# Background weights by Pool's queue into three places, with four smaller edits, in a two-layer hybrid trunk

## The chip, the cores and the metric

The kernel runs as one program on one core of a Trainium2 chip. The metric is the device time of one execution in microseconds; before the change it was measured three times. TensorE (PE) does the matrix products, VectorE (DVE) and ScalarE (ACT) the elementwise work, GpSimd (POOL) a few small operations, and SyncE (SP) issues the transfers. Each engine runs its own instructions in order.

## The reference

Two layers of one mixer over 256 latent tokens and 256 context tokens of width 2048, batch 1, all in float32. The second layer needs the context only for keys and values. Cut to what matters here (the rotary positions of q and k are left out):

```python
for l in range(2):
    shift, scale, gate = split(silu(c) @ w_mod[l] + b_mod[l])        # and the same of c_ctx for the context
    h = rmsnorm(x, norm_g[l]) * (1 + scale) + shift
    q, k, v, g_att, u_pool, g_pool, a, b, g_conv = split(h @ w_in[l])  # 2048 -> 6656
    # 8 heads, each with two softmaxes over context and latent keys
    p = softmax(q @ k.T * 64 ** -0.5)
    o = (p[0] - lam * p[1]) @ v
    y_att = rmsnorm(o, subln_g) * (1 - lam_init) * silu(g_att)
    y_pool = multiscale_pool(u_pool) * silu(g_pool)
    y_conv = conformer_conv(a, b) * silu(g_conv)
    x = x + gate * (concat(y_att, y_pool, y_conv) @ w_out[l])
return rmsnorm(x, final_g)
```

## The kernel before

Activations lie with the channels on the 128 partitions and the tokens (512, or 256 in layer 1) along the free side: the residual is 16 tiles `s0` to `s15`. To keep float32 accuracy each operand is split into a high part in the float32r form and a low part that is the rest (ScalarE casts, VectorE subtracts), and each product is three matmuls: high by high, low by high, high by low. The names end in `h` and `l`: `hh`, `hl` are the normalised input, `in_q_h`, `in_q_l` weights of a chunk of q, from the loaded `in_q_r`. The input projection is done chunk by chunk (`b0 a0 q0 k0 v0 u0 b1 ...`, 256 columns each, 16 tiles of the inner dimension), each into two banks of PSUM (`ps_q`, `ps_v`, ...).

**The first stage.** The x tiles are loaded, squared on ScalarE and added up on VectorE (`add_squares`); TensorE sums over the channels (`rms_sum`, line 178), GpSimd takes the power -1/2 (line 145), TensorE spreads the root over the partitions (line 160), and ScalarE copies it (`rstd`). Meanwhile the modulation of layer 0 (shift and scale) is made on TensorE from 512 KB pieces `wm` (line 336, `modacc`); each finished pair is turned by a small matmul (`modt`) and finished on VectorE (`modsum`, `mod`). Each tile of `h`, `hh`, `hl` then feeds the first three chunks at once (`ps_first`, three held pairs of banks), as their weights `first_*` come. The order within this stage is written out by hand: inside `in_order()` each engine keeps the order of the code.

**The background.** The gates of layer 0 and the whole modulation of layer 1 are made on VectorE, by `mod_on_dve`: 8 units of 1024 columns in 16 pieces each, 128 loads `mraw` of 128x1024 and 224 multiply-accumulates `macc` (line 370 the first of a unit, line 372 the others; two for each piece where latent and context rows are both wanted, one otherwise). Its places rotate under the tag `mraw`, `MRAW` of them; the first stage's `wm` pieces use the same tag for two of every eight. A load for piece n+1 is issued when the macc of piece n is written, into the place that macc n-1 has left:

```python
        for n in range(MRAW - 1):
            load(n)
        yield 0.0
        for n, (l, u, both, k) in enumerate(pieces):
            load(n + MRAW - 1)
            raw = raws.popleft()
```

**Attention** (`attention`, one pair of heads) is a generator too. After the scores, `softmax` takes the negative maximum (`mx`, line 634), two exponentials with sums (line 640), the reciprocal `r` of both sums (line 644), multiplies the second by minus lambda (line 645), scales the first part on ScalarE (line 648) and adds the second on VectorE (line 649); TensorE then transposes the result `ex` into `atx` (line 684). At the end of a pair the squares of the head outputs are summed (`ssq`) and rooted by three Newton steps on VectorE (`arw`, lines 152 to 154) into a kept tile `arv`. Later, when the gate chunk `ga` is projected, `gate_att` splits that root, spreads it with eight matmuls (`ar`), multiplies the head by it (line 761) and by the silu of the gate (line 762).

A scheduler interleaves the generators with the projection chunks: each `yield` gives the microseconds of VectorE work that a step is taken to be, and every projection step of `FULL` hands that much out. So the numbers at the `yield`s set where on VectorE the maccs and the attention's steps stand.

## Time and profile before

| what | value |
|---|---|
| three runs | 1498.68, 1493.88, 1495.42 us, median 1495.42 |
| profiled execution | 1502.84 us, its span 1501.0 us |
| mean granted TensorE clock | 0.992 |
| TensorE busy | 1452.5 us, 97% |
| VectorE busy | 1112.8 us, 74% |
| ScalarE busy | 650.2 us, 43% |
| GpSimd busy | 9.0 us, 1% |
| transfers | 258.9 MB, nearly all by SyncE's queue |

The time of a run is that of the whole execution; the span of the profile is from the first instruction to the last, and all times below count from its start. The profiled execution is a run of its own, 7.4 us above the median of the other three. "Busy" of TensorE counts the time that a matmul is in its pipeline, at whatever clock.

### The profile page before, as it was taken

Reading aid. Unit: us, or ns where it says so; the run is one execution under the profiler, and the core shown is the slowest. Engines: PE = TensorE matmul, PEld = TensorE weight load, DVE = VectorE, ACT = ScalarE, POOL = GpSimd, SP = SyncE. Lnnn points to the kernel's source line nnn. Section 1 sums busy time; section 2 is a strip of 40 time slices with the busy share of each in tenths; the row PEclk is TensorE's granted clock in tenths of the full one; section 3 lists DMA queues with packets and bytes.
Section 4 is the critical chain, followed back from the end, with each engine's and each line's share of the span. In section 5 each row is a group of like instructions: output and inputs, shape, how many; then the busy total and the mean of one; then the engine's idle time right before and its main releaser. Section 6 shows DMA issues by size and latency. Waiting matters only on the chain.

```text
span 1501.0 us, 23277 instructions
## 1 busy us (share of the span) xinstructions
PE 1452.5 (97%) x9196; PEld 1241.8 (83%) x9196; DVE 1112.8 (74%) x1641; ACT 650.2 (43%) x1245; POOL 9.0 (1%) x46
## 2 busy tenths in 40 slices
PE   4999999999999999999999999999999999999997
PEld 3567977897797977888888889988989897999997
DVE  4446999997549865879898964998995567475655
ACT  4224363227546363332433242635545545464543
POOL 0000000000000000000000000000000000000000
PEclk9999999999999999999999999999999999999998
DMA  8995226432234613655667761436733264245553
GB/s 332 397 391 221 81 88 202 148 110 74 74 112 146 202 60 113 221 195 203 209 213 250 243 222 55 142 114 216 265 113 124 79 227 161 99 134 178 187 183 113
DMA packets 75855, 258.90 MB, mean 172 GB/s; under 512 B 8800, under 2 KB 11104, under 8 KB 75744
## 3 DMA queue, kind: packets, MB, share of 16 engines
q1 hardware_dynamic: 75456, 257.14, 49.2%
q8 instruction: 72, 1.18, 0.3%
q14 instruction: 39, 0.32, 0.1%
q10 hardware_dynamic: 288, 0.26, 0.1%
HBM read 255.27 MB, written 2.10 MB: 171 GB/s over the span
## 4 chain that ended last, share of the span: by engine, by line
PE 83%; DVE 7%; DMA 4%; issue 3%; ACT 2%; SPq 0%; POOL 0%; POOLq 0%; DVEq 0%; ACTq 0%
PE ps_o L236 16%; PE ps_k L236 12%; PE ps_ga L236 9%; PE ps_v L227 7%; PE ps_q L236 6%; PE ps_gc L236 5%; PE ps_gp L236 4%; PE ps_first L236 4%; PE ps_b L236 3%; PE ps_u L236 3%; PE ps_a L236 3%; DMA mraw<-in_w_mod 3%; PE modacc L336 2%; DVE s L479 2%; DVE macc L372 1%
## 5 line engine op out<-in xcount | busy, mean ns | idle before, releaser
L372 DVE SCALAR_TENSOR_TENSOR macc<-mraw,c_sb,macc 128x1024 f32<-128x1024 f32 x210 | 262.6, 1280 | 32.2 <-DMA mraw<-in_w_mod 31.5
L236 PE MATMUL ps_o<-yh,out_h 128*128 128x512 f32 (+1 forms) x448 | 151.7, 339 | 0.0
L236 PE MATMUL ps_o<-yl,out_h 128*128 128x512 f32 (+1 forms) x448 | 151.6, 338 | 0.0
L236 PE MATMUL ps_o<-yh,out_l 128*128 128x512 f32 (+1 forms) x448 | 151.6, 338 | 0.0
L227 PE MATMUL ps_v<-in_v_h,hh 128*128 128x256 f32 x512 | 145.2, 284 | 0.0
L227 PE MATMUL ps_v<-in_v_h,hl 128*128 128x256 f32 x512 | 144.8, 283 | 0.0
L227 PE MATMUL ps_v<-in_v_l,hh 128*128 128x256 f32 x512 | 144.3, 282 | 0.0
L479 DVE SCALAR_TENSOR_TENSOR s<-cu,vec,s 128x512 f32<-128x512 f32 (+1 forms) x240 | 136.5, 615 | 0.5
L205 ACT CAST out_h<-out_r 128x1024 fp32r<-128x1024 f32 x56 | 58.8, 1050 | 111.5 <-PE ps_o L236 97.2
L236 PE MATMUL ps_k<-hh,in_k_h 128*128 128x512 f32 x256 | 102.9, 402 | 1.9 <-ACT ex L640 1.0
L236 PE MATMUL ps_k<-hl,in_k_h 128*128 128x512 f32 x256 | 102.1, 399 | 0.0
L236 PE MATMUL ps_k<-hh,in_k_l 128*128 128x512 f32 x256 | 101.8, 398 | 0.0
L227 PEld LDWEIGHTS ps_v<-in_v_l,hh 128*128 128x128 f32 x512 | 96.7, 189 | 0.3
L227 PEld LDWEIGHTS ps_v<-in_v_h,hh 128*128 128x128 f32 x512 | 96.7, 189 | 0.3
L227 PEld LDWEIGHTS ps_v<-in_v_h,hl 128*128 128x128 f32 x512 | 96.4, 188 | 0.0
L236 PEld LDWEIGHTS ps_o<-yl,out_h 128*128 128x128 f32 x448 | 84.3, 188 | 9.9
L236 PEld LDWEIGHTS ps_o<-yh,out_h 128*128 128x128 f32 x448 | 84.3, 188 | 9.9
L236 PEld LDWEIGHTS ps_o<-yh,out_l 128*128 128x128 f32 x448 | 84.3, 188 | 9.8
L206 DVE TENSOR_TENSOR out_l<-out_r,out_h 128x1024 fp32r<-128x1024 f32 x56 | 68.1, 1223 | 32.1 <-ACT out_h L205 30.7
L236 PE MATMUL ps_ga<-hh,in_ga_h 128*128 128x512 f32 (+1 forms) x256 | 87.2, 340 | 1.0 <-ACT ex L640 1.0
L236 PE MATMUL ps_ga<-hl,in_ga_h 128*128 128x512 f32 (+1 forms) x256 | 87.0, 340 | 0.0
L236 PE MATMUL ps_ga<-hh,in_ga_l 128*128 128x512 f32 (+1 forms) x256 | 87.0, 340 | 0.0
(407 smaller groups left out, 3708.2 us busy)
## 6 DMA issues: line engine op xcount, KB each, us to landing
mraw<-in_w_mod SPq DMA_DIRECT2D x128, 512.0 KB, 4.3
wm<-in_w_mod SPq DMA_DIRECT2D x64, 512.0 KB, 8.5
out_r<-in_w_out SPq DMA_DIRECT2D x56, 512.0 KB, 4.0
in_k_r<-in_w_in SPq DMA_DIRECT2D x32, 512.0 KB, 4.4
in_v_r<-in_w_in SPq DMA_DIRECT2D x32, 512.0 KB, 3.4
in_ga_r<-in_w_in SPq DMA_DIRECT2D x32, 512.0 KB, 3.8
in_q_r<-in_w_in SPq DMA_DIRECT2D x28, 512.0 KB, 3.5
in_u_r<-in_w_in SPq DMA_DIRECT2D x16, 512.0 KB, 3.4
```

The lines of the kernel that those rows point to most:

```text
L205: nc.scalar.copy(out=hi, in_=raw)
L206: nc.vector.tensor_sub(out=lo, in0=raw, in1=hi.bitcast(F32))
L227: nc.tensor.matmul(o, lhsT=a[:, ts], rhs=b[:, j, :], start=f and n == 0 and tt % 2 == 0, stop=e and n == 2, skip_group_check=True,)
L236: nc.tensor.matmul(ps[:, nt, t0:t1], lhsT=a[:, j, ns], rhs=b[:, t0:t1], start=f and n == 0, stop=e and n == 2,)
L336: nc.tensor.matmul(acc[c : c + 32, :n], lhsT=sc32[:, k, :], rhs=raw[:, j, :], start=k < 4, stop=k >= KT - 4, skip_group_check=True,)
L372: nc.vector.scalar_tensor_tensor(out=acc[:, r, :], in0=raw, scalar=sc[:, k, r : r + 1], in1=acc[:, r, :], op0=ALU.mult, op1=ALU.add)
L479: nc.vector.scalar_tensor_tensor(out=acc, in0=u[:, :nq, j : j + TL], scalar=w[:, j : j + 1], in1=acc, op0=ALU.mult, op1=ALU.add)
```

## The change

1. **Loads of the background** go from SyncE's queue to GpSimd's, and `MRAW` is 3 instead of 2: two loads are written ahead, and a load waits for the macc two pieces before its own but one (load n+2 for macc n-1). The third `mraw` place is there for the first stage's `wm` too.
2. **Heads' normalisation**: the split of the root, its eight matmuls and the product with the head move from `gate_att` to the end of `attention`, which gets a step of 1.2; `gate_att` keeps the silu and one product.
3. **Softmax**: the second reciprocal is multiplied by minus lambda on ScalarE, ahead of the scaling there, no longer on VectorE.
4. **First stage**: `ident` and `vec0` are loaded behind the tenth x tile; squares are added in pairs of tiles (six adds of 128x1024, three of 128x512, before fifteen of 128x512); sums and spread use a held bank of `ps_first`; TensorE does the sums, three modulation pieces, the spread, the fourth piece.
5. **Its end**: `take` (the GLU, pooling or rotary steps that follow a chunk) of the first three chunks is called right behind the last product of each.

```diff
-MRAW = 2
+MRAW = 3
...
-                nc.sync.dma_start(out=raw, in_=w_mod[6 * l + u - 4, k])
+                nc.gpsimd.dma_start(out=raw, in_=w_mod[6 * l + u - 4, k])
...
-        nc.vector.tensor_scalar(out=r[:, 1, :], in0=r[:, 1, :], scalar1=L.neglam, scalar2=None, op0=ALU.mult)
+        nc.scalar.activation(r[:, 1, :], r[:, 1, :], AF.Copy, scale=L.neglam)
...
-        v = one.tile([P, TL], F32, tag=f"arv{p}", name=f"arv{l}_{p}")[:, :nh]
+        work = tmp(f"arw{l}_{p}")
+        v, a, y = work[:, :nh], work[:, TL : TL + nh], tmp(f"ary{l}_{p}")[:, :nh]
         nc.vector.tensor_scalar(out=v, in0=b, scalar1=1.0 / P, scalar2=EPS, op0=ALU.mult, op1=ALU.add)
...
-    def gate_att(L, p, ps):
...
-        split_act(hi, lo, L.arstd[p])
+        split_act(hi, lo, v)
+        yield 4.0
         for h in range(2):
...
+            o = L.y[2 * p + h]
+            nc.vector.scalar_tensor_tensor(out=o, in0=o, scalar=L.subg, in1=r, op0=ALU.mult, op1=ALU.mult)
+        L.arstd[p] = True
+        yield 1.2
...
-            nc.vector.scalar_tensor_tensor(out=y, in0=y, scalar=L.subg, in1=r, op0=ALU.mult, op1=ALU.mult)
             nc.vector.tensor_tensor(out=y, in0=y, in1=g[:, :n], op=ALU.mult)
...
+    def last_product(k, i):
+        product(k, i)
+        if k == KT - 1:
+            take(L, ORDER[i], held[i])
...
             nc.sync.dma_start(out=s[k], in_=xT[k])
+            if k == 9:
+                small_loads()
...
-        add_squares(s, sq_acc, "xsq")
+        both = mp.tile([P, 2, 1024], F32, tag="macc", name="xsq", bufs=1)[:, 0, :]
+        for k in range(0, KT - 2, 2):
+            q = both if k == 0 else at.tile([P, 1024], F32, tag=("vh", "vl", "ah", "al")[k // 2 % 4], name=f"xsq{k}")
+            for i in range(2):
+                nc.scalar.activation(q[:, i * T : (i + 1) * T], s[k + i], AF.Square)
+            if k:
+                nc.vector.tensor_tensor(out=both, in0=both, in1=q, op=ALU.add)
...
+        y = rstd_of([sq_acc], 4, 1.0 / D, "rms0", held[2][:, 0, :])
         steps = mod_on_pe(0)
-        next(steps)
-        next(steps)
-        y = rstd_of([sq_acc], 4, 1.0 / D, "rms0")
+        for _ in range(3):
+            next(steps)
         finishes.popleft()()
-        next(steps)
-        next(steps)
-        r0 = spread(y, "rms0")
+        r0 = spread(y, "rms0", held[2][:, 1, :])
```

**Where instructions stand now.** VectorE in layer 1 ahead of the first softmax of head 4 (`mxx_4_0`, `rx_4_0`), before; `macc_5` is the unit with its pieces `mraw_5_0` to `mraw_5_15`, the rest are splits of weights:

```order
L372 SCALAR_TENSOR_TENSOR macc_5_11107<-mraw_5_7_11232,c_sb,macc_5_11107 128x1024
L206 TENSOR_TENSOR in_q_3_l<-in_q_3_r,in_q_3_h 128x1024
L372 SCALAR_TENSOR_TENSOR macc_5_11107<-mraw_5_8_11235,c_sb,macc_5_11107 128x1024
L634 TENSOR_REDUCE mxx_4_0_11343<-sx_4_0_11336 128x2
L372 SCALAR_TENSOR_TENSOR macc_5_11107<-mraw_5_9_11292,c_sb,macc_5_11107 128x1024
L206 TENSOR_TENSOR in_q_2_l<-in_q_2_r,in_q_2_h 128x1024
L634 TENSOR_REDUCE mxx_4_1_11391<-sx_4_1_11384 128x2
L372 SCALAR_TENSOR_TENSOR macc_5_11107<-mraw_5_10_11295,c_sb,macc_5_11107 128x1024
L644 RECIPROCAL rx_4_0_11349<-ssx_4_0_11346 128x2
L206 TENSOR_TENSOR in_k_0_l<-in_k_0_r,in_k_0_h 128x1024
L645 TENSOR_SCALAR rx_4_0_11349<-rx_4_0_11349,neglam_8163 128x1
```

The same place after the change. Piece 13 stands ahead of the reciprocal `rx_4_0` where piece 10 did, and line 645's product is gone from VectorE. Ahead of the layer's first reciprocal it is piece 9 where it was piece 7:

```order
L374 SCALAR_TENSOR_TENSOR macc_5_11110<-mraw_5_10_11295,c_sb,macc_5_11110 128x1024
L215 TENSOR_TENSOR vl_2_11305<-ps_v_1_11042,vh_2_11304 128x1024
L208 TENSOR_TENSOR in_q_3_l<-in_q_3_r,in_q_3_h 128x1024
L374 SCALAR_TENSOR_TENSOR macc_5_11110<-mraw_5_11_11298,c_sb,macc_5_11110 128x1024
L636 TENSOR_REDUCE mxx_4_0_11346<-sx_4_0_11339 128x2
L208 TENSOR_TENSOR in_q_2_l<-in_q_2_r,in_q_2_h 128x1024
L374 SCALAR_TENSOR_TENSOR macc_5_11110<-mraw_5_12_11301,c_sb,macc_5_11110 128x1024
L374 SCALAR_TENSOR_TENSOR macc_5_11110<-mraw_5_13_11642,c_sb,macc_5_11110 128x1024
L646 RECIPROCAL rx_4_0_11352<-ssx_4_0_11349 128x2
L636 TENSOR_REDUCE mxx_4_1_11394<-sx_4_1_11387 128x2
L651 SCALAR_TENSOR_TENSOR ex_4_0_11348<-ex_4_0_11348,rx_4_0_11352 128x512
```

VectorE at the end of the first stage, before: the last tile's `h_15`, its second modulation, and `hl_15`, with the lambda's steps and the first macc behind it.

```order
L411 SCALAR_TENSOR_TENSOR h_15_1278<-s_106,mod_118,rstd_305 128x256 x2
L206 TENSOR_TENSOR in_k_3_l<-in_k_3_r,in_k_3_h 128x1024
L326 TENSOR_REDUCE modsum_15_1308<-modt_15_1306 128x2
L290 TENSOR_TENSOR mod_118<-modsum_15_1308,vec_84 128x2
L422 SCALAR_TENSOR_TENSOR hl_15_152<-h_15_1278,mod_118,hh_15_151 128x256 x2
L828 TENSOR_TENSOR lam_1339<-lam_1339 128x128
L830 TENSOR_REDUCE lams_1342<-lam_1339 128x2
L370 TENSOR_SCALAR macc_4_2285<-mraw_4_0_2281,c_sb 128x1024
```

The same after: two line-372 products and one macc (line 374) stand between `h_15` and `hl_15`, three maccs more behind it, and lambda's steps have moved back.

```order
L413 SCALAR_TENSOR_TENSOR h_15_1264<-s_106,mod_115,rstd_279 128x256 x2
L372 TENSOR_SCALAR macc_4_2318<-mraw_4_0_2312,c_sb 128x1024
L208 TENSOR_TENSOR in_k_3_l<-in_k_3_r,in_k_3_h 128x1024
L328 TENSOR_REDUCE modsum_15_1294<-modt_15_1292 128x2
L372 TENSOR_SCALAR macc_4_2318<-mraw_4_0_2312,c_sb 128x1024
L292 TENSOR_TENSOR mod_115<-modsum_15_1294,vec_84 128x2
L374 SCALAR_TENSOR_TENSOR macc_4_2318<-mraw_4_1_2314,c_sb,macc_4_2318 128x1024
L424 SCALAR_TENSOR_TENSOR hl_15_149<-h_15_1264,mod_115,hh_15_148 128x256 x2
L374 SCALAR_TENSOR_TENSOR macc_4_2318<-mraw_4_1_2314,c_sb,macc_4_2318 128x1024
L374 SCALAR_TENSOR_TENSOR macc_4_2318<-mraw_4_2_2316,c_sb,macc_4_2318 128x1024 x2
```

TensorE at the start, before (`wm_0_0` and `wm_0_1` are pieces of the first modulation, `ps_first` with `first_0` the first product):

```order
L336 MATMUL modacc_0_240<-wm_0_0_172,sc_115 32x128 x8
L336 MATMUL modacc_0_240<-wm_0_1_174,sc_115 32x128 x8
L178 MATMUL rms_sum<-ones,sq_acc 128x1 x4
L323 MATMUL modt_0_271<-ident,modrow_0_261 128x128
L336 MATMUL modacc_0_277<-wm_0_0_176,sc_115 32x128 x8
L336 MATMUL modacc_0_277<-wm_0_1_178,sc_115 32x128 x8
L160 MATMUL rms_rstd<-ident,rms_v 128x128 x4
L323 MATMUL modt_0_310<-ident,modrow_0_298 128x128
L236 MATMUL ps_first_153<-hh_0_121,first_0_0qh 128x512
```

After: the sums (line 180) come first and the spread (line 162) stands behind three pieces and the turn.

```order
L180 MATMUL ps_first_152<-ones,sq_acc 128x1 x4
L338 MATMUL modacc_0_235<-wm_0_0_171,sc_112 32x128 x8
L338 MATMUL modacc_0_235<-wm_0_1_173,sc_112 32x128 x8
L338 MATMUL modacc_0_258<-wm_0_0_175,sc_112 32x128 x8
L325 MATMUL modt_0_269<-ident,modrow_0_256 128x128
L162 MATMUL ps_first_152<-ident,rms_v 128x128 x4
L338 MATMUL modacc_0_258<-wm_0_1_177,sc_112 32x128 x8
L325 MATMUL modt_0_296<-ident,modrow_0_291 128x128
L238 MATMUL ps_first_150<-hh_0_118,first_0_0qh 128x512
```

## Rows read from the trace of the kernel before

**Rows 1.** The page, part 1: busy time, share of the span and instructions of each engine.

```profile
PE 1452.5 (97%) x9196; PEld 1241.8 (83%) x9196; DVE 1112.8 (74%) x1641; ACT 650.2 (43%) x1245; POOL 9.0 (1%) x46
```

**Rows 2.** The page, part 4: the chain that ended last, shares of the span.

```profile
PE 83%; DVE 7%; DMA 4%; issue 3%; ACT 2%; SPq 0%; POOL 0%; POOLq 0%; DVEq 0%; ACTq 0%
```

**Rows 3.** Windows: busy time of each engine, then granted clock, DMA share, GB/s.

```profile
50.00:75.00 25.00, 22.86 (x186) 14.51 (x179) 11.55 (x27) 7.68 (x15) 0.00 (x0) 1.00 1.02 406
150.00:200.00 50.00, 49.47 (x317) 43.62 (x315) 49.86 (x68) 19.04 (x27) 0.00 (x0) 1.00 0.28 96
600.00:925.00 325.00, 325.00 (x1495) 264.82 (x1494) 263.71 (x277) 106.94 (x262) 0.31 (x4) 1.00 0.62 209
1225.00:1250.00 25.00, 21.39 (x156) 18.27 (x155) 20.33 (x24) 13.38 (x22) 0.00 (x0) 0.94 0.74 246
```

**Rows 4.** Waits of the whole span: total us, times, longest us.

```profile
DVE macc L372 <- DMA mraw<-in_w_mod: 31.5, 39, 2.0
...
PE atx L684 <- DVE ex L649: 8.5, 5, 3.6
```

**Rows 5.** Timeline of TensorE in layer 1: start, us, instruction, idle time before.

```profile
1034.69 0.66 PE L684 MATMUL atx<-ident,ex 128*128 128x128 f32 x4 [2.56 <-DVE ex L649]
...
1246.36 0.66 PE L684 MATMUL atx<-ident,ex 128*128 128x128 f32 x4 [3.61 <-DVE ex L649]
```

**Rows 6.** Windows of layer 1 just behind those two, columns as in rows 3.

```profile
1035.49:1038.91 3.42, 3.42 (x18) 3.42 (x18) 3.42 (x7) 2.09 (x6) 0.00 (x0) 0.50 0.59 189
1247.12:1253.95 6.83, 6.83 (x21) 4.50 (x20) 6.06 (x10) 5.45 (x12) 0.00 (x0) 0.50 0.53 190
```

**Rows 7.** Tile mraw, with the page's part 6 for wm (last column: us to landing).

```profile
L372 DVE SCALAR_TENSOR_TENSOR macc<-mraw,c_sb,macc x210: 1257/1280/1287, 189.5 to 1263.7; 128x1024 f32<-128x1024 f32 x105
...
L370 DVE TENSOR_SCALAR macc<-mraw,c_sb x14: 746/751/754, 136.4 to 1211.4; 128x1024 f32<-128x1024 f32 x14
...
DMA to landing us min/median/max: 3.3/4.3/6.6
...
wm<-in_w_mod SPq DMA_DIRECT2D x64, 512.0 KB, 8.5
```

**Rows 8.** Timeline of VectorE, layer 1, first stretch.

```profile
1008.55 0.75 DVE L370 TENSOR_SCALAR macc<-mraw,c_sb 128x1024 f32<-128x1024 f32 x1
...
1014.74 1.28 DVE L372 SCALAR_TENSOR_TENSOR macc<-mraw,c_sb,macc 128x1024 f32<-128x1024 f32 x1 [1.80 <-DMA mraw<-in_w_mod]
...
1030.24 1.28 DVE L372 SCALAR_TENSOR_TENSOR macc<-mraw,c_sb,macc 128x1024 f32<-128x1024 f32 x1 [1.26 <-DMA mraw<-in_w_mod]
...
1031.44 0.16 DVE L644 RECIPROCAL rx<-ssx 128x2 f32<-128x2 f32 x1
```

**Rows 9.** Timeline of VectorE, layer 1, second stretch.

```profile
1213.27 1.28 DVE L372 SCALAR_TENSOR_TENSOR macc<-mraw,c_sb,macc 128x1024 f32<-128x1024 f32 x1
1215.73 1.29 DVE L372 SCALAR_TENSOR_TENSOR macc<-mraw,c_sb,macc 128x1024 f32<-128x1024 f32 x1 [1.18 <-DMA mraw<-in_w_mod]
...
1241.85 1.28 DVE L372 SCALAR_TENSOR_TENSOR macc<-mraw,c_sb,macc 128x1024 f32<-128x1024 f32 x1 [1.45 <-DMA mraw<-in_w_mod]
1243.05 0.15 DVE L644 RECIPROCAL rx<-ssx 128x2 f32<-128x2 f32 x1
```

**Rows 10.** Timeline of the first stage, all engines.

```profile
17.28 2.27 PE L336 MATMUL modacc<-wm,sc 128*32 128x128 f32 x32 [17.28 <-DMA wm<-in_w_mod]
...
25.45 0.58 ACT L890 COPY rstd<-rms_rstd 128x512 f32<-128x512 f32 x1 [1.58 <-PE rms_rstd L160]
...
29.15 0.80 PE L236 MATMUL ps_first<-hh,first_0qh 128*128 128x512 f32 x1 [3.63 <-ACT first_0qh L205]
```

**Rows 11.** Timeline of VectorE at the first stage's end.

```profile
134.77 0.88 DVE L422 SCALAR_TENSOR_TENSOR hl<-h,mod,hh 128x256 fp32r<-128x256 f32 x2 [0.58 <-ACT hh L421]
```

**Rows 12.** Lines 645 and 761: duration ns min/median/max, first and last start.

```profile
L645 DVE TENSOR_SCALAR rx<-rx,neglam x32: 202/214/226, 197.9 to 1324.3; 128x1 f32<-128x1 f32 x32
...
L761 DVE SCALAR_TENSOR_TENSOR s<-s,subg,ar x12: 472/610/749, 586.8 to 1377.0; 128x512 f32<-128x512 f32 x6, 128x256 f32<-128x256 f32 x6
```

More of the change, by code (lines that the diff above doesn't have):

```diff
@@ L125, in trunk, with small_loads @@
     nc.gpsimd.memset(half, -0.5)
+    def small_loads():
+        nc.sync.dma_start(out=ident, in_=eye)
+        nc.sync.dma_start(out=vec[0], in_=vecs[0])
     def late_loads():
@@ L135, in trunk @@
     ident_r = one.tile([P, P], F32R, name="ident_r")
-    nc.vector.tensor_copy(out=ident_r, in_=ident)
     sc32 = utile("sc32", [P, KT, 32])
@@ L759, in gate_att @@
                     )
+            o = L.y[2 * p + h]
+            nc.vector.scalar_tensor_tensor(out=o, in0=o, scalar=L.subg, in1=r, op0=ALU.mult, op1=ALU.mult)
+        L.arstd[p] = True
+        yield 1.2
+    def gate_att(L, p, ps):
+        n, l = L.n, L.l
+        for h in range(2):
+            head = 2 * p + h
+            g = tmp(f"sga{l}_{head}")
+            nc.scalar.activation(g[:, :n], ps[:, h, :n], AF.Silu)
             y = L.y[head]
-            nc.vector.scalar_tensor_tensor(out=y, in0=y, scalar=L.subg, in1=r, op0=ALU.mult, op1=ALU.mult)
             nc.vector.tensor_tensor(out=y, in0=y, in1=g[:, :n], op=ALU.mult)
@@ L879, in first_stage @@
         mod_fetch(4)
-        add_squares(s, sq_acc, "xsq")
+        both = mp.tile([P, 2, 1024], F32, tag="macc", name="xsq", bufs=1)[:, 0, :]
[5 more added lines that the diff above has]
+                nc.vector.tensor_tensor(out=both, in0=both, in1=q, op=ALU.add)
+        nc.vector.tensor_tensor(out=sq_acc, in0=both[:, :T], in1=both[:, T:], op=ALU.add)
+        for k in (KT - 2, KT - 1):
+            q = tmp(f"xsq{k}")
+            nc.scalar.activation(q, s[k], AF.Square)
+            nc.vector.tensor_tensor(out=sq_acc, in0=sq_acc, in1=q, op=ALU.add)
+        nc.vector.tensor_copy(out=ident_r, in_=ident)
+        y = rstd_of([sq_acc], 4, 1.0 / D, "rms0", held[2][:, 0, :])
         steps = mod_on_pe(0)
-        next(steps)
-        next(steps)
-        y = rstd_of([sq_acc], 4, 1.0 / D, "rms0")
+        for _ in range(3):
+            next(steps)
         finishes.popleft()()
-        next(steps)
-        next(steps)
-        r0 = spread(y, "rms0")
+        r0 = spread(y, "rms0", held[2][:, 1, :])
         rstd = mp.tile([P, 2, 1024], F32, tag="macc", name="rstd0", bufs=1)[:, 0, :T]
         nc.scalar.copy(out=rstd, in_=r0)
+        next(steps)
         scaled = {0: first_scaled(0, rstd)}
@@ L926, in first_stage @@
             if now:
-                product(*now.popleft())
+                last_product(*now.popleft())
             elif more:
@@ L936, in first_stage @@
             while now:
-                product(*now.popleft())
+                last_product(*now.popleft())
             for _ in steps:
@@ L943, in trunk @@
     prepare(L)
-    for i in range(START):
-        take(L, ORDER[i], held[i])
     mod_work.append(mod_on_dve([(0, 4, True), (0, 5, True)] + [(1, u, True) for u in range(4)]))
```

26 lines of the change are left out of this document (8 added, 18 removed).

## The prediction

> **What bounds the kernel now.** I read the page's first part, then the chain that ended last, the waits, the stretches where TensorE falls idle, and the timelines of those. TensorE is busy 97% of the span and VectorE 74% [rows 1]; the chain runs through TensorE for 83%, VectorE for 7% and DMA for 4% [rows 2]. So a change pays only in the few places where TensorE waits, or runs at a low clock. From 600 to 925 us TensorE is busy for all 325 us, so whatever waits there costs nothing; from 150 to 200 us VectorE is full as well, 49.86 of 50 us, with TensorE still at 49.47; from 1225 to 1250 TensorE works for only 21.39 of 25 us [rows 3].
>
> The wait that this change aims at is the longest of those with a DMA behind them on VectorE: a multiply-accumulate of the background modulation (`macc`) waits for its weights (`mraw`) 39 times, 31.5 us in all, never over 2.0 us [rows 4]. Most of that must be free, since TensorE has only 1501.0 - 1452.5 = 48.5 us without a matmul, all causes together. Where it is not free can be read in layer 1. There the last reductions of a softmax stand behind maccs on VectorE, in order, and TensorE waits for the softmax's result `ex` (line 649): five waits, 8.5 us, the longest 3.6 [rows 4]. Two of them are 2.56 us before 1034.69 and 3.61 us before 1246.36 [rows 5]. Right behind each the granted clock is 0.50 (the 1.2 GHz level) for 3.42 and 6.83 us, with TensorE busy all through [rows 6]; half of that time, 1.7 and 3.4 us, is lost too. So the two places cost 2.56 + 3.61 + 5.1 = 11.3 us.
>
> **Weights by the Pool queue, three places.** 128 loads of 512 KB leave SyncE's queue. With two places, load n+1 starts when macc n-1 ends, and with a landing time L two maccs take 1.28 + L. With three places it is three maccs. L was 3.3 to 6.6 us, median 4.3, from SyncE [rows 7]. No load went by Pool's queue before, so its L is unknown. I bound it by 3.3 below and, above, by the 8.5 us of the first stage's weights on full queues [rows 7].
>
> The three-macc planning also moves maccs forward: ahead of the first reciprocal of layer 1 stand 10 instead of 8, ahead of that of head 4 stand 14 instead of 11. A macc behind another costs 1.20 us (1241.85 to 1243.05 [rows 9]).
>
> First stretch: from macc 0 at 1008.55 to the reciprocal at 1031.44, VectorE waits five times for `mraw`, from 1.80 to 1.26 us, 5.3 us together [rows 8]. Without waits and with two more maccs the reciprocal comes at 1031.44 - 5.3 + 2.4 = 1028.5. The loads allow it no earlier than macc 9, three rounds behind macc 0: 1008.55 + 0.75 + L + 2(1.28 + L) + 1.28 = 1013.1 + 3L. For L up to 5.1 the work decides, and the reciprocal is 2.9 us earlier; at L = 6.1 nothing is gained; at 6.6 it is 1.5 us late.
>
> Second stretch: seven waits between 1213.27 and 1243.05, 1.18 to 1.45 us, sum 6.4 [rows 9]; three more maccs cost 3.6. By work: 1243.05 - 6.4 + 3.6 = 1240.25, 2.8 us earlier. By loads: macc 13 is four rounds behind macc 1, 1213.27 + 4(1.28 + L) + 1.28 = 1219.7 + 4L: again L = 5.1 is where loads begin to decide, 5.85 where the gain is gone, and 6.6 costs 3.0.
>
> I take L = 5: nearer to the 4.3 of the same transfer than to the 8.5, since here the queues aren't full, and a little longer for another issuer. Then the stalls shrink by 2.56 and 2.8 = 5.4 us. Of the clock's 5.1 I count half, 2.6, because 0.8 us of the second stall and the smaller atx waits stay. Term: **-8.0**, between -11.3 (both places clean) and +17.8 (L = 8.5: 7.2 + 10.6 late); at L = 6.6 it is +4.5.
>
> A rule of the Trainium skill speaks against this part (SBUF — State Buffer, Who interferes with whom): descriptors of a DMA issued from GpSimd are written by its cores, which are locked out while VectorE runs a copy, cast or tensor_scalar in a two-port mode; it advises the SyncE or ScalarE queue. By it L would grow; but of a like operation with two tensor inputs it says that it has no such mode, and the rows show the maccs as 210 scalar_tensor_tensors of 1.28 us and 14 tensor_scalars of 0.75 [rows 7]: by the trace the lock would seldom be held. The Trainium skill's page DMA: Bandwidth & Descriptors (Anatomy of one DMA) gives 2.0 us plus bytes/436e3 for a Pool-issued load; an estimate from it is 3.2 us for 512 KB, and the sum would then be that of L = 5 or a little better.
>
> SyncE's other loads no longer stand behind waits for a macc's place. ScalarE's casts wait mostly for TensorE's release of their buffers, not for the loads, so: 0. Pool has 9.0 us of work in all [rows 1]; its few `pow` stand among the loads, in the order of the maccs: 0.
>
> **The first stage.** Two small loads behind the x tiles, squares by pairs and another order: the sums no longer stand behind two modulation pieces (2.27 us from 17.28 [rows 10]), but three pieces now stand between sums and spread, where one pair stood; and the cast of the first product's weights runs ahead of `hh_0` rather than behind it. The first product starts at 29.15 after a 3.63 us wait for that cast, ScalarE's copy of the roots at 25.45 [rows 10]. The best is the 2.2 us of the two pieces, the least 0, as the second product waits for `hl_0`, now behind a split of weights on VectorE, and everything up to 125 us takes its weights through DMA engines that are full (share 1.02 in 50 to 75, where TensorE already waits 2.1 us [rows 3]). I take **-1.0**.
>
> At this stage's end the order puts two tensor_scalars and a macc between `h_15` and `hl_15`: 2 x 0.75 + 1.28 = 2.8 us ahead of an operation that ran at 134.77 [rows 11] and that the last products wait for. Some of it fits into VectorE's idle time. I take **+1.5**, between 0 and +2.8.
>
> **Softmax and head normalisation.** 40 tensor_scalars, the 32 of 0.21 us and 8 like them, leave VectorE [rows 12]; a like operation on ScalarE now stands in the chain from the reciprocal to `ex`. Five TensorE waits there at 0.2 us are +1.0 at most; against it VectorE gets at most 40 x 0.21 = 8.4 us back, which counts only where it is full (a quarter, 2 us, at best), and the maccs leave the stretches of heads 2 to 5 of layer 0. I take **-0.5**, -2 to +1. The 16 products with the heads' roots (the 12 and 4 like them, median 0.61 us [rows 12]) and the ar matmuls move from the gate to the end of attention. Before, TensorE's gate products hid them; now VectorE's next work hides or pays them. If the cover is gone it is at most 4.9 us of VectorE per layer, half of it on TensorE: 0 to +2.5. I take **0**.
>
> **Sum.** -8.0 - 1.0 + 1.5 - 0.5 = -8.0 us. The profiled execution took 1502.84 us, 7.4 above the median of 1495.42; the sum gives 1494.8 for a profiled one and **1487.4** for the median. 0.3%, about what can be told from no change here, is 4.5 us.
>
> **Rivals.** (1) *Loads by Pool land late.* If a load takes longer by this queue, then from L = 6 the maccs, now more of them ahead of the reductions, hold the softmax of layer 1 up longer than before. At 6.6 the first term is +4.5 instead of -8.0 and the time 1499.9; at 8.5 it is 1513. For it: no row shows such a load, and 6.6 has occurred. Against: the median of 4.3, and a DMA share of only 0.74 in the second stretch [rows 3]. Slower; chance 0.17.
> (2) *The gain doesn't reach TensorE.* The waits go, but the softmax then waits on ScalarE (its exponents end just before) or the clock falls all the same, so that at most 2 us remain, eaten by the first stage's end: 1493 to 1497. For it: 31.5 us of waits against 48.5 us of all idle time. Chance 0.22.
> (3) *VectorE becomes the bound in layer 0.* Two more maccs (2.4 us) stand ahead of the first maxima where VectorE is full, and the moved normalisation adds its 2.5: 1487.4 + 4.9 = 1492.3. Chance 0.10, between faster and same.
> (4) *Both places clean*, no low clock: another 3.3 us and no loss at 135 us: 1483 or less. Chance 0.15.
> The forecast itself, 1484 to 1491: 0.36.
>
> **How the numbers follow.** Faster than 1490.9: the forecast, (4), a third of (3) and a little of (2)'s lower edge: 0.36 + 0.15 + 0.03 + 0.03 = 0.57. Within 0.3%: the rest of (2) and (3), 0.19 + 0.06 = 0.25. Slower than 1499.9: (1), and 0.01 of (3), 0.18. The range goes from 1480 (all gains at their far end: 1487.4 - 3.3 - 1.2 - 1.5 - 1.5) to 1500 (L = 6.6); the forecast's own is 1484 to 1491.
>
> **What would show it.** Right: the landing time of `mraw` below 5.2 us, VectorE's waits for it under 12 us, the two atx waits of 2.56 and 3.61 us under 1 us, no stretch at 0.50 near 1035 and 1247, the first product near 28. Wrong: landing above 5.9, waits for `mraw` still near 30 us, the low clock in the same places or in new ones, a wait of over 2 us at 135, VectorE's waits for `ar` or for the scaled factor grown by several us.

## The result, and the profile after

The change made the kernel slower: 1506.39 us median of five runs (1503.62 to 1508.36) against 1495.42 of five of the kernel before (1493.88 to 1499.63), a ratio of 1.0068 [1.0054, 1.0082], about 10 us. The prediction was 1487.4. The profiled execution took 1503.62 us, the shortest of the five, so its trace shows less than the whole loss.

The page's part 1 answers to [rows 1]. TensorE is as busy as before; GpSimd's 9.0 us became 77.4, since issuing a load now counts there.

```profile
PE 1452.6 (97%) x9196; PEld 1240.8 (83%) x9196; DVE 1109.0 (74%) x1595; ACT 657.7 (44%) x1284; POOL 77.4 (5%) x174
```

The waits of the whole span answer to [rows 4]: total us, times, longest.

```profile
DVE macc L374 <- DMA mraw<-in_w_mod: 12.1, 11, 3.9
...
PE atx L686 <- DVE ex L651: 7.7, 5, 3.5
```

VectorE waits for `mraw` 11 times instead of 39, 12.1 us instead of 31.5, near the forecast of under 12. But the longest wait grew from 2.0 to 3.9 us, and TensorE's waits for `ex` only fell from 8.5 to 7.7 us. Tile `mraw`, answering to [rows 7]:

```profile
L358 POOL DMA_DIRECT2D mraw<-in_w_mod x128: 527/527/711, 110.2 to 1242.6; - x128
...
DMA to landing us min/median/max: 3.6/4.5/8.3
```

The median landing rose by 0.2 us, the longest from 6.6 to 8.3. (The 8.3 is the load of 110.2 us, for which nothing waited.) What one long landing does is seen in layer 1's second stretch. VectorE's timeline, answering to [rows 9], with GpSimd's and SyncE's rows of the same stretch:

```profile
1211.02 0.75 DVE L372 TENSOR_SCALAR macc<-mraw,c_sb 128x1024 f32<-128x1024 f32 x1 [2.08 <-PE modt L385]
...
1215.99 1.28 DVE L374 SCALAR_TENSOR_TENSOR macc<-mraw,c_sb,macc 128x1024 f32<-128x1024 f32 x1 [0.49 <-DMA mraw<-in_w_mod]
...
1217.68 0.53 POOL L358 DMA_DIRECT2D mraw<-in_w_mod  x1 [1.25 <-DVE macc L374]
...
1220.33 0.53 POOL L358 DMA_DIRECT2D mraw<-in_w_mod  x1 [2.12 <-DVE macc L374]
1221.09 0.33 SPq L191 DMA_DIRECT2D in_k_r<-in_w_in  x1
...
1227.87 1.28 DVE L374 SCALAR_TENSOR_TENSOR macc<-mraw,c_sb,macc 128x1024 f32<-128x1024 f32 x1 [3.86 <-DMA mraw<-in_w_mod]
...
1243.43 0.16 DVE L646 RECIPROCAL rx<-ssx 128x2 f32<-128x2 f32 x1
```

The load issued at 1220.33 takes 7.4 us, and the macc that needs it waits 3.86 us, to 1227.87. SyncE had issued a 512 KB load of `in_k_r` 0.76 us behind it. The first reciprocal comes 32.4 us after macc 0 (1243.43 - 1211.02); in between VectorE waits six times for `mraw`, 7.2 us in all with that one. The rows show one more thing: the macc of 1215.99 ends at 1217.27, and the load that may then start is issued at 1217.68, 0.41 us later. Before, the macc of 1213.27 ended at 1214.55 [rows 9], and SyncE's timeline of that kernel has its load 0.03 us later:

```profile
1214.58 2.79 SPq L356 DMA_DIRECT2D mraw<-in_w_mod  x2
```

TensorE's timeline, answering to [rows 5] and [rows 10]: the stalls for `ex` are 2.58 and 3.52 us, before 2.56 and 3.61.

```profile
28.29 0.49 PE L238 MATMUL ps_first<-hh,first_0qh 128*128 128x512 f32 x1 [1.42 <-ACT hh L423]
...
134.31 0.51 PE L238 MATMUL ps_first<-hh,first_0e 128*128 128x512 f32 x1 [1.11 <-ACT hh L423]
135.36 0.50 PE L238 MATMUL ps_first<-hl,first_0e 128*128 128x512 f32 x1 [0.54 <-DVE hl L424]
...
1031.93 0.66 PE L686 MATMUL atx<-ident,ex 128*128 128x128 f32 x4 [2.58 <-DVE ex L651]
...
1245.42 1.11 PE L686 MATMUL atx<-ident,ex 128*128 128x128 f32 x4 [3.52 <-DVE ex L651]
```

Windows, columns as in [rows 3]. From 1225 to 1250 TensorE works for 18.94 us, before for 21.39; behind the stall the granted clock is 0.50 (1.2 GHz) again [rows 6].

```profile
125.00:150.00 25.00, 23.35 (x154) 17.84 (x154) 23.05 (x40) 12.56 (x19) 2.29 (x6) 1.00 0.48 157
...
1225.00:1250.00 25.00, 18.94 (x129) 16.19 (x129) 20.98 (x21) 11.84 (x20) 3.16 (x6) 0.89 0.72 260
...
1245.00:1250.00 5.00, 4.58 (x18) 3.50 (x19) 5.00 (x7) 4.00 (x9) 0.00 (x0) 0.50 0.51 186
```

### The profile page after: what moved, and what is told of

Read it like the earlier page. It is cut to its first block, busy times and chain, and to the rows that moved or that the text cites. A ratio compares the mean times of both kernels' runs of the same rounds, so it can differ in the third digit from the quotient of the medians.

```text
span 1501.8 us, 23295 instructions
## 1 busy us (share of the span) xinstructions
PE 1452.6 (97%) x9196; PEld 1240.8 (83%) x9196; DVE 1109.0 (74%) x1595; ACT 657.7 (44%) x1284; POOL 77.4 (5%) x174
## 3 DMA queue, kind: packets, MB, share of 16 engines
q8 instruction: 72, 1.18, 0.3%
## 4 chain that ended last, share of the span: by engine, by line
PE 82%; issue 7%; DVE 6%; DMA 3%; ACT 2%; POOL 0%; SPq 0%; POOLq 0%; DVEq 0%; ACTq 0%
PE ps_o L238 16%; PE ps_k L238 10%; PE ps_ga L238 9%; PE ps_v L229 8%; PE ps_q L238 6%; PE ps_gp L238 4%; PE ps_gc L238 4%; PE ps_first L238 4%; PE ps_u L238 3%; PE ps_b L238 3%; PE ps_a L238 2%; DMA mraw<-in_w_mod 2%; PE modacc L338 2%; PE sx L662 1%; DVE macc L374 1%
## 5 line engine op out<-in xcount | busy, mean ns | idle before, releaser
L374 DVE SCALAR_TENSOR_TENSOR macc<-mraw,c_sb,macc 128x1024 f32<-128x1024 f32 x210 | 261.7, 1282 | 12.3 <-DMA mraw<-in_w_mod 12.1
L207 ACT CAST out_h<-out_r 128x1024 fp32r<-128x1024 f32 x56 | 58.8, 1050 | 127.7 <-PE ps_o L238 116.1
L358 POOL DMA_DIRECT2D mraw<-in_w_mod x128 | 68.1, 532 | 848.2 <-DVE macc L374 360.8
```

The lines of the kernel that those rows point to most:

```text
L207: nc.scalar.copy(out=hi, in_=raw)
L358: nc.gpsimd.dma_start(out=raw, in_=w_mod[6 * l + u - 4, k])
L374: nc.vector.scalar_tensor_tensor(out=acc[:, r, :], in0=raw, scalar=sc[:, k, r : r + 1], in1=acc[:, r, :], op0=ALU.mult, op1=ALU.add)
```

## The experiments

The ratios are to the kernel before, run beside it on the same chip. The first theory was that GpSimd's queue carries the loss, by late loads. The rivals were the moved normalisation, and the order of the instructions, which a scheduler makes and which changes when only the queue changes: between the changed kernel and the same kernel with its loads on SyncE's queue, 235 of VectorE's 1595 places hold another instruction.

**c_before.** The kernel before, unchanged.

> The kernel before, unchanged, as a control and for a second trace. The first trace of it took 1502.84 us, 7.4 above the median of its runs, while the trace of the changed kernel (1503.62) is at the low end of its own runs; so the two traces look alike and the medians differ by 11 us. Theory A (the loss is in the places where a trace varies: the stalls and low clock at 1035 and 1247): a second trace of about 1495 lacks one of these places. Theory B (the 7 us are outside the stalls, spread out): the second trace has the same waits of TensorE, and differs in nothing that a view shows. Ratio expected 1.000 +- 0.002.

0.9997 [0.9984, 1.0010]. Its trace has a span of 1492.3 us where the first profile had 1501.0. TensorE's timeline and the windows of the two stretches:

```profile
1032.59 0.65 PE L684 MATMUL atx<-ident,ex 128*128 128x128 f32 x4 [1.72 <-DVE ex L649]
...
1240.99 0.66 PE L684 MATMUL atx<-ident,ex 128*128 128x128 f32 x4 [2.35 <-DVE ex L649]
...
1030.00:1055.00 25.00, 23.24 (x183) 20.71 (x182) 23.41 (x41) 15.97 (x33) 0.00 (x0) 1.00 0.66 206
1225.00:1250.00 25.00, 22.63 (x157) 19.03 (x156) 23.18 (x31) 16.53 (x32) 0.00 (x0) 1.00 0.74 233
```

The waits for `mraw` are those of [rows 4] (32.3 us, 40 times), but the stalls are 1.72 and 2.35 us and the granted clock stays at 1.00. Of the 11.3 us that the prediction found in these places, 4.1 are left in this execution. At 1494.05 us it is the shortest of the control's twelve (median 1496.22), as the first profile, at 1502.84, was longer than all five runs of the kernel before; a typical run lies between the two, nearer to this one.

**q_pool_two_places.** The queue alone, with two places.

```diff
-                nc.sync.dma_start(out=raw, in_=w_mod[6 * l + u - 4, k])
+                nc.gpsimd.dma_start(out=raw, in_=w_mod[6 * l + u - 4, k])
```

> The kernel before with the background loads on GpSimd's queue alone; two places as before. Theory queue (a load by this queue lands later, with a longer tail: 4.5 us in the middle and 8.3 at most in the changed kernel, 4.3 and 6.6 before): waits of VectorE for mraw grow from 31.5 to over 36 us, and the time grows by 4 to 10 us. Theory order (the queue is harmless, the denser maccs of three places are what costs): within 2 us of before, waits 30 to 36 us.

1.0147 [1.0130, 1.0164], +22 us: the costliest edit by itself, and over twice what was expected of it. VectorE waits 66.3 us for `mraw` in 50 waits (before 31.5 in 39).

**x_pool_old_order** and **x_sp_pool_order** take the queue and the order apart. The kernel is built twice; the order of TensorE, VectorE and ScalarE from the first build is forced on the second, which has the other queue. In the traces the three engines' instructions follow one another in the forced order.

```diff
+                getattr(nc, QUEUE).dma_start(out=raw, in_=w_mod[6 * l + u - 4, k])
...
+                    if traced[b].engine == traced[a].engine:
+                        tc.add_manual_dep(
+                            traced[b], names[a],
...
+    order = build("sync")[2]
...
+    nc, feed, done = build(BUILD_QUEUE, {k: v for k, v in order.items() if k in ENGINES})
```

> Background loads on GpSimd's queue with two places, but TensorE, VectorE and ScalarE held to the very order of the kernel before (no instruction of theirs moves). Loads on GpSimd's queue alone cost 22 us, and there VectorE's waits for mraw grew from 32 to 66 us; but that kernel's order differed from before too, since the scheduler puts the maccs elsewhere when the loads are on another queue. Theory transport (a load starts 0.4 us after its place is free instead of 0.03, and some land after 6 to 8 us): most of the 22 us are here too, +12 to +22, waits near 60 us. Theory order (the moved maccs cost it): +0 to +6 here, waits 45 to 55 us.

1.0149 [1.0119, 1.0180]: GpSimd's queue with the order of before costs as much as the queue alone, 76.1 us of waits for `mraw` in 54. (The trace is of a run of 1529.89 us, 11 above the median of the six, so a typical run waits less.) One of its long landings, in the transfers issued from 250.5 to 251.5 us (last column: us to landing):

```profile
mraw<-in_w_mod POOLq DMA_DIRECT2D x1, 512.0 KB, 7.5
in_q_r<-in_w_in SPq DMA_DIRECT2D x1, 512.0 KB, 6.9
```

> The counterpart: loads on SyncE's queue as before, but TensorE, VectorE and ScalarE in the order that the scheduler gives when they are on GpSimd's queue. Theory order: +12 to +20 us, waits for mraw over 45 us though the loads come by SyncE, and TensorE's 2.8 us wait for hl_15 at 135 us. Theory transport: within 5 us of before.

1.0079 [1.0063, 1.0095]: that order on SyncE's queue, with two places, costs 12 us by itself. Half of it is one stall of TensorE, 5.58 us at 142 us, for the last tile of `hh`, whose modulation stands on VectorE behind a macc that waits 4.5 us for its load. VectorE's waits for `mraw` are 36.6 us, not the 45 that theory order wanted. The two costs, 22 and 12 us, don't add up: both together are the 22 of q_pool_two_places.

**n_norm_alone** and **n_norm_three_places.** The second edit of the change alone, then with the third place, on SyncE's queue.

```diff
-MRAW = 2
+MRAW = 3            # only in n_norm_three_places
...
+            o = L.y[2 * p + h]
+            nc.vector.scalar_tensor_tensor(out=o, in0=o, scalar=L.subg, in1=r, op0=ALU.mult, op1=ALU.mult)
+        L.arstd[p] = True
+        yield 1.2
```

> The kernel before with the heads' normalisation at the end of attention alone. Theory norm (VectorE's work moves into stretches where it is full; ScalarE waited 20.6 us for the root in the changed kernel): +3 to +8 us. Theory order or queue: within 2 us of before.

1.0043 [1.0027, 1.0058], +6.4 us. TensorE's timeline shows stalls that the control has not (there it waits 0.64 us at most in 536 to 546, and from 1050 to 1075 it is busy for all 25.00 us):

```profile
543.00 1.11 PE L684 MATMUL atx<-ident,ex 128*128 128x128 f32 x4 [2.75 <-DVE ex L649]
...
1067.25 1.21 PE L748 MATMUL ar<-arp,ident_r 128*128 128x128 f32 x8 [0.58 <-ACT arp L212]
1069.96 0.35 PE L586 MATMUL pool<-pdh,wpool_h 128*128 128x256 f32 x1 [1.21 <-DVE s L753]
```

The `ar` matmuls and the product with the head (line 753 here) are now waited for, where the gate's products had hidden them.

> The heads' normalisation at the end of attention (which frees the room) and three places, loads on SyncE's queue. The normalisation alone is +6.5 us. Theory (three places take the waits away): VectorE's waits for mraw from 25 to under 10 us and -2 to -6 us against the normalisation alone, so +0 to +4 against before. Theory (the denser maccs stand ahead of the reductions and cost what the waits gave): +6 to +10 against before.

0.9990 [0.9977, 1.0003]: with the third place the two edits together are worth -1.5 us. VectorE's waits for `mraw` fall to 4.7 us in 7.

**f_first_alone**, **s_softmax_alone** and **t_take_alone**: the fourth, third and fifth edit, each alone.

```diff
+            if k == 9:
+                small_loads()
...
-        nc.vector.tensor_scalar(out=r[:, 1, :], in0=r[:, 1, :], scalar1=L.neglam, scalar2=None, op0=ALU.mult)
+        nc.scalar.activation(r[:, 1, :], r[:, 1, :], AF.Copy, scale=L.neglam)
...
+        if k == KT - 1:
+            take(L, ORDER[i], held[i])
```

> The kernel before with the new first stage alone (small loads behind the tenth tile, squares by pairs, the sums ahead of the modulation pieces, cast ahead of hh_0), its end as before. In the changed kernel TensorE's first matmul comes at 18.58 instead of 17.28 and the first product at 28.2 instead of 29.15. Theory first (the sums ahead hold back the modulation pieces, whose weights have landed): 0 to +2 us. By the prediction's term: -1.0.

0.9988 [0.9976, 1.0000], -1.8 us.

> The kernel before with the second reciprocal's factor on ScalarE alone. In the changed kernel the small activation takes 0.29 us and stands in the chain between the reciprocal and the scaling. Prediction's term: -0.5, between -2 and +1. A rival: the scheduler's order shifts with it and the layer 1 stalls move by a few us either way; then up to +-4.

0.9997 [0.9987, 1.0008]: nothing.

> The kernel before with one edit of the change alone: take of the first three chunks is called right behind the last product of each. If the term of the prediction holds (two tensor_scalars and a macc between h_15 and hl_15, +1.5, between 0 and +2.8): 1496 to 1499 us, ratio 1.000 to 1.002, TensorE waits of 1.5 to 2.5 us near 133 us. If VectorE's idle time there hides it: 1494 to 1496, ratio 0.999 to 1.000, no such wait.

1.0007 [0.9995, 1.0018]; TensorE has no stall between 128 and 140 us. So the 1.11 and 0.54 us at 134 in the changed kernel are not due to this edit alone.

**a_on_sp.** The changed kernel with its loads back on SyncE's queue.

```diff
-                nc.gpsimd.dma_start(out=raw, in_=w_mod[6 * l + u - 4, k])
+                nc.sync.dma_start(out=raw, in_=w_mod[6 * l + u - 4, k])
```

> The changed kernel with its background loads back on SyncE's queue, three places and all else kept. Theory queue (transport or order, what the queue brings): half or more of the +11 us goes: +0 to +5 against before. Theory normalisation: the queue is harmless with three places, +8 to +11 stays.

0.9972 [0.9960, 0.9983]: faster than both kernels, by 4.2 us than the one before and, ratio against ratio, by 14 us than the changed one. Its waits:

```profile
DVE macc L374 <- DMA mraw<-in_w_mod: 3.9, 7, 0.9
...
PE atx L686 <- DVE ex L651: 4.1, 5, 1.2
```

**b_nonorm_three_sp.** The same with the normalisation at the gate as before, which leaves room for three places of `raw` (weights before their split) instead of four.

```diff
-        raw = wp.tile([P, 1024], F32, tag="raw", name=f"{name}_r", bufs=4)
+        raw = wp.tile([P, 1024], F32, tag="raw", name=f"{name}_r", bufs=3)
```

> The changed kernel with its loads on SyncE's queue, three places for mraw, and the heads' normalisation back at the gate; the room comes from the raw weights, three places instead of four. With the normalisation moved this version without the last two edits is -4.2 us against before, and the normalisation alone cost +6.5 with two places. Theory (the normalisation's cost stays in it): -7 to -12 us, the fastest so far. Theory (three places absorb that cost, since the maccs no longer crowd the end of attention): -2 to -5. Against both: the raw weights' lost place makes ScalarE's casts wait for loads, +0 or worse.

0.9981 [0.9969, 0.9994]: not told apart from a_on_sp. So the third place and the moved normalisation are not separate terms: the moved normalisation costs 6.4 us with two places, and with three no cost is seen. This last comparison isn't clean, as `raw` has one place less here too.

**y_pool_sp_order** and **y_sp_pool_order.** The changed kernel's two queues and two orders, crossed by the same forcing.

> The changed kernel with its loads on Pool's queue and three places, but TensorE, VectorE and ScalarE held to the order of instructions of the kernel a_on_sp (the same change with the loads on SyncE's queue, 0.9972 of the time before). It has the transport of the changed kernel and not its order. Theory T (the transport by the second queue costs what separates the changed kernel, 1506.4, from a_on_sp, 1493.9): 1503 to 1508 us, ratio 1.004 to 1.008, longest landing of mraw over 7.5 us. Theory O (the order that the scheduler makes when the queue changes costs it): 1492 to 1497, ratio 0.996 to 1.000, with the same long landings. A half each: about 1500, ratio 1.003.

1.0021 [1.0008, 1.0034]: the queue with the order of a_on_sp costs 7 us more than a_on_sp (0.0049 of the time), and the changed kernel's own order another 7 (0.0047).

> The changed kernel with its loads on SyncE's queue and three places, TensorE, VectorE and ScalarE held to the order of the changed kernel as it was timed. It has that order and not its transport. Theory T: 1492 to 1497 us, ratio 0.996 to 1.000, longest landing of mraw below 7.2 us, waits of macc for mraw below 6 us. Theory O: 1503 to 1508, ratio 1.004 to 1.008. With two places that order cost 12.3 us on SyncE's queue, because one early wait of 5.7 us came at 136 us; a third place should take away that wait, so T is the likelier.

1.0053 [1.0036, 1.0069]: the order on SyncE's queue costs 12 us, where theory T had at most 0. Its longest landing is 8.7 us and its waits for `mraw` are over 10, all on SyncE's queue, where theory T wanted below 7.2 and below 6. Its trace says why, in the timeline of all engines and the windows:

```profile
128.76 1.37 SPq L359 DMA_DIRECT2D mraw<-in_w_mod  x3
...
135.49 0.75 DVE L373 TENSOR_SCALAR macc<-mraw,c_sb 128x1024 f32<-128x1024 f32 x1 [4.84 <-DMA mraw<-in_w_mod]
...
139.18 0.79 PE L239 MATMUL ps_first<-hh,first_0e 128*128 128x512 f32 x1 [5.92 <-ACT hh L424]
...
125.00:150.00 25.00, 18.83 (x125) 13.99 (x124) 16.22 (x27) 8.97 (x14) 0.18 (x2) 0.86 0.55 195
```

SyncE reaches the first `mraw` loads at 128.76, behind the weights in its queue (GpSimd: 110.2), and maccs stand on VectorE ahead of what `hh` of the last tile needs; TensorE waits 5.92 us. Six of the 12 us are idle time in this one place (18.83 us busy of 25, in a_on_sp 24.89), and the clock of 0.86 there is an estimated 3.5 more (0.14 of 25); the changed kernel does not have this place. In layer 1's second stretch the two causes add up in the time of the reciprocal. VectorE's timelines, from macc 0 to the first reciprocal, of a_on_sp:

```profile
1208.88 0.75 DVE L372 TENSOR_SCALAR macc<-mraw,c_sb 128x1024 f32<-128x1024 f32 x1 [2.15 <-PE modt L385]
...
1236.28 0.16 DVE L646 RECIPROCAL rx<-ssx 128x2 f32<-128x2 f32 x1
```

of y_pool_sp_order:

```profile
1208.47 0.75 DVE L373 TENSOR_SCALAR macc<-mraw,c_sb 128x1024 f32<-128x1024 f32 x1 [2.14 <-PE modt L386]
...
1229.74 1.28 DVE L375 SCALAR_TENSOR_TENSOR macc<-mraw,c_sb,macc 128x1024 f32<-128x1024 f32 x1 [3.18 <-DMA mraw<-in_w_mod]
...
1239.18 0.16 DVE L647 RECIPROCAL rx<-ssx 128x2 f32<-128x2 f32 x1
```

and of y_sp_pool_order:

```profile
1215.47 0.75 DVE L373 TENSOR_SCALAR macc<-mraw,c_sb 128x1024 f32<-128x1024 f32 x1 [2.08 <-PE modt L386]
...
1245.10 0.16 DVE L647 RECIPROCAL rx<-ssx 128x2 f32<-128x2 f32 x1
```

| macc 0 to the first reciprocal, us | order of a_on_sp (13 maccs) | order of the changed kernel (14) |
|---|---|---|
| SyncE's queue | 27.4 | 29.6 |
| GpSimd's queue | 30.7 | 32.4 |

The queue adds 2.8 to 3.3 us and the order 1.7 to 2.2. VectorE's waits for `mraw` in the stretch are 2.0 us in a_on_sp, 6.5 with the queue, 4.4 with the order and 7.2 with both; the longest of them are 3.18 and 3.86 us by GpSimd's queue. The order also has one macc more (1.20 us, [rows 9]).

TensorE's stall behind the reciprocal does not add up so. It is 1.2 us in a_on_sp and 3.5 in the changed kernel, and either cause alone takes it to 3.3 or 3.4, as the waits of y_pool_sp_order and of y_sp_pool_order show:

```profile
PE atx L687 <- DVE ex L652: 7.2, 5, 3.3
...
PE atx L687 <- DVE ex L652: 6.1, 6, 3.4
```

This stretch holds most of what the traces of a_on_sp and of the changed kernel differ by (spans of 1492.1 and 1501.8 us). The window of a_on_sp:

```profile
1225.00:1250.00 25.00, 23.79 (x167) 20.02 (x167) 24.37 (x26) 17.66 (x34) 0.00 (x0) 1.00 0.70 238
```

The changed kernel has 18.94 us at 0.89 there: 4.9 us less work, and an estimated 2.8 lost to the clock (0.11 of 25). The clock counts in the whole time too. Over the runs of one kernel some 1 us goes with 0.001 of the mean granted clock (an estimate over all runs; the control's extremes are 1494.05 us at 0.998 and 1502.62 at 0.992). The changed kernel's five runs have 0.991 to 0.994 and the control's twelve 0.992 to 0.998, so by this estimate about a third of the ten us is work done at the lower clock, mostly behind such stalls.

**x_all_pool_old_order.** Both kinds of loads, `mraw` and the split weights, on GpSimd's queue, two places, the order of before.

```diff
-        nc.sync.dma_start(out=raw[:, : shape[1] * shape[2]].rearrange("p (k n) -> p k n", n=shape[2]), in_=src)
+        getattr(nc, QUEUE).dma_start(out=raw[:, : shape[1] * shape[2]].rearrange("p (k n) -> p k n", n=shape[2]), in_=src)
```

> As the run that holds the three engines to the order of before with the background loads on GpSimd's queue (+21.7 us, landing up to 8.3 us), but with the split weights' 512 KB loads on GpSimd's queue too, so that one queue carries both kinds again. In the trace of the former each slow mraw load (over 6.3 us) has a load of SyncE's queue issued 0.7 to 0.9 us behind it, which is slow too. Theory collision (two loads on two queues at the same time slow each other, one queue takes them one after the other): the long landings go (median 4 to 4.6, maximum under 6), VectorE's waits for mraw fall from 76 to 40 to 55 us, and the time is +3 to +10. Theory slow start (each load by GpSimd's queue pays for its 0.4 us and its own issue): waits stay over 65 us, +18 us or more.

1.0074 [1.0062, 1.0086], against 1.0149 with the loads on two queues. The longest landing of `mraw` falls from 8.3 to 6.8 us, and landings over 6 us from 18 to 1. So half the cost at two places is not GpSimd's queue as such but the second queue beside the first. What the other 11 us are, no run takes apart; the later issue, 0.41 against 0.03 us for each load, is a candidate.

**m_pairs** and **m_triples.** Loads with nothing else in flight, the kernel's work left out: in pairs, then in threes (the code of the threes).

```diff
+                for who, t in zip(kind, (t1, p2, p3)):
+                    q = nc.sync if who == "s" else nc.gpsimd
+                    q.dma_start(out=t, in_=w_mod[n % 8, (n // 8) % KT])
```

> Only pairs of 512 KB loads, the rest of the computation left out (the output is not the reference's). The first load starts when a VectorE add has written its place, the second after 0, 0.1, 0.5, 1.1, 2.3 or 4.5 us more of adds (letters a to f); ss both by SyncE, ps first by GpSimd and second by SyncE, sp the other way, pp both by GpSimd. Theory collision: in ps, with gaps c and d, both take over 6 us to land, and with f the first takes about 3.6; in ss the first takes 3.4 at every gap and the second at most 4.6. Theory slow start: ps's first takes the same time at every gap, and never over 5.

No pair came near the long landings: at most 4.9 us (median), with GpSimd's load first and SyncE's 0.2 us behind it. That miss left the cause open until the threes.

> Leaves out the whole computation: only groups of three loads of 512 KB with nothing else in flight, on SyncE's (s) and Pool's (p) queue as sss, pps, ppp and sps, the second 0, 1.2, 2.6 and 2.6 us behind the first, the third about 0.6 us (1.2 in the last) behind the second; its time says nothing of the kernel. Theory Q (loads on two queues share the DMA engines load by load, so that all in flight end late, while one queue serves them in turn): in pps the second and the third land after 6 us or more, in sss and ppp the first two after 3.3 to 4.5 and only the third later. Theory B (only the bytes in flight count): the sum of the three landings is the same in pps, sss and ppp within 1 us, and no second load of pps takes over 5.5 us.

The transfers of m_triples (last column: median us to landing of four), for the gaps of the second set:

```profile
onesssb<-in_w_mod SPq DMA_DIRECT2D x4, 512.0 KB, 3.3
twosssb<-in_w_mod SPq DMA_DIRECT2D x4, 512.0 KB, 4.8
threesssb<-in_w_mod SPq DMA_DIRECT2D x4, 512.0 KB, 5.4
...
threeppsb<-in_w_mod SPq DMA_DIRECT2D x4, 512.0 KB, 7.1
...
oneppsb<-in_w_mod POOLq DMA_DIRECT2D x4, 512.0 KB, 3.6
twoppsb<-in_w_mod POOLq DMA_DIRECT2D x4, 512.0 KB, 7.1
...
onepppb<-in_w_mod POOLq DMA_DIRECT2D x4, 512.0 KB, 3.6
twopppb<-in_w_mod POOLq DMA_DIRECT2D x4, 512.0 KB, 5.1
...
threepppb<-in_w_mod POOLq DMA_DIRECT2D x4, 512.0 KB, 5.8
```

Two loads from GpSimd and one from SyncE within 2 us: the second and the third take 7.1 us each. Three by one queue, either one, take at most 5.8 (medians of four; single ones reached 6.9). The gaps are not quite the same, as the third comes 0.2 us behind the second in the mixed set and 0.6 in the others; but counted from the first issue all three are there after 8.4 us in the mixed set and after 7.1 and 7.5 in the others, so it is not only the bytes. Two by SyncE and one by GpSimd between them take 3.3, 6.0 and 6.0. Theory Q holds in the first set too: there the load named `two` is issued 1.2 us ahead of `one` and takes 3.6, the other two 6.9 and 6.7.

Where the second comes 2.6 us after the first, both fall to 5.1, and with another 0.5 us between second and third to 3.6 and 4.1:

```profile
twoppsd<-in_w_mod POOLq DMA_DIRECT2D x4, 512.0 KB, 3.6
...
threeppsd<-in_w_mod SPq DMA_DIRECT2D x4, 512.0 KB, 4.1
```

These last are the gaps of the changed kernel's long load (2.65 us behind one of GpSimd's, SyncE's 0.76 behind it), so m_triples does not show 7 us at the kernel's own gaps. What differs is that there the load ahead took 4.9 us itself and had 2.3 still to go; in the set with 7.1 us it had 2.5, in the last one 1.0. The kernels' traces have it at their own gaps. Take the `mraw` loads that find an earlier load with 2.0 us or more to go and have a load of weights issued 0.3 to 1.3 us behind them: in the four traces with two queues 52 of 67 take over 6 us (in the changed kernel 12 of 17), in the twelve with one queue 4 of 123.

## Why the prediction was wrong

**The queue: the step that failed.** The prediction took one landing time for all loads, L = 5, and asked from which L on the loads decide. The median was 4.5, so by that sum the gain was safe. But a chain of 14 maccs waits for the worst of its loads, not the median. Without the one wait of 3.86 us the reciprocal would have come 28.5 us after macc 0 (32.4 - 3.9), and the sum by work had 28.9 (1240.25, with macc 0 at 1211.4 [rows 7]); but this is luck. The stretch waits 7.2 us for `mraw`, where the sum by work had nothing, and has 25.2 us of the rest instead of 28.9, since VectorE's three waits for ScalarE's casts in the kernel before (2.6 us, which the prediction counted as work) and one maximum are gone from it. (The seven waits that the prediction gives as 1.18 to 1.45 us go from 0.41 to 1.45; their sum is right.)

The long load is rival 1 in its mechanism, at 7.4 us instead of 6.6 and in single loads. What the sum had not priced is the collision: with SyncE's weights and GpSimd's `mraw` in flight together single loads take 7 us and more, as the transfers of x_pool_old_order, m_triples and the counts show. The queue with its order cost 14 us (1.0068 against 0.9972). In the order of a_on_sp the queue alone costs 7; in the changed kernel's order it adds 2 (1.0068 against 1.0053), as that order has its own late place on SyncE's queue. So the 14 us are shown for the two together, and their shares depend on which is changed first.

The Trainium skill has a reason for long landings on this queue (SBUF — State Buffer, Who interferes with whom), VectorE's two-port operations. It advised SyncE's queue and was right in the result, but that lock isn't needed: in m_triples VectorE sits idle for the 7.14 us until the load is there.

```profile
317.45 1.23 DVE L108 TENSOR_TENSOR acc<-oneppsb,twoppsb 128x1024 f32<-128x1024 f32 x1 [7.14 <-DMA twoppsb<-in_w_mod]
```

Nearer to these rows is the Trainium skill's page DMA: Bandwidth & Descriptors (Queues, rings and completion order): each DMA engine takes the queues that have work in turn, a packet from each. That agrees with two loads ending together, 7.1 us each with 0.2 us between their issues, and 7.4 and 6.9 with 0.76 in the changed kernel; why they also end later than two in one queue, no run here shows.

**The order.** The prediction read from the order that three more maccs stand ahead of head 4's reciprocal, and charged them to the third place. On SyncE's queue the scheduler puts 13 there, not 14: a part of the new order is due to the queue alone, here and elsewhere, and on GpSimd's queue it cost 7 us (1.0068 against 1.0021). The +1.5 at the first stage's end is there (1.11 + 0.54 us at 134), but it too comes with that order: with GpSimd's queue and the order of a_on_sp TensorE is busy for 24.89 us from 125 to 150, in the changed kernel for 23.35.

**The gain that was priced.** The term of -8.0 was read from stalls and low clock of one execution, 7.4 us above the median; the prediction noted the offset and still took 8.0 of the 11.3 us found there as won. The control's trace, of its shortest run, has 4.1 us there. In a_on_sp, on SyncE's queue, the two stalls fall from 1.72 and 2.35 to 1.19 each: 1.7 us.

**Normalisation: mis-sized.** Priced at 0 (0 to +2.5), it costs 6.4 alone, of which 2.75, 0.58 and 1.21 us are the stalls shown. The cover that the prediction named, VectorE's next work, pays for it only with the third place there: -1.5 for both, where the sum had -8.0.

**The small terms** are not contradicted: first stage -1.8 (forecast -1.0; first product at 28.29, forecast near 28), softmax nothing (-0.5). `take` alone is +1.0, which its interval does not tell from nothing.

By measured terms: queue with its order +14.4, places and normalisation -1.5, first stage -1.8, `take` +1.0, softmax -0.4: +11.7, measured +10.2. The first of these is itself read from the changed kernel; what the sum tests is the rest, -2.7, against the -4.2 of a_on_sp.

## What to carry to other kernels

Where a chain of loads feeds an engine in order, price it by the worst landing beside everything else in flight, and keep background loads on the queue that the other loads use unless a run shows otherwise. A scheduler reads the queue too: changing it changed three engines' order, so cross the queue and the order before blaming either. Before pricing a stall, see it in a second trace of the same kernel: a profile 0.5% above the median may hold just the stalls that one goes after.
